# Later feed-forwards on 256 normed columns, and rows placed 64 bytes below the weights

## The chip, the cores and the metric

The kernel runs on one core of a Trainium2 chip. The metric is the device time of one execution in microseconds, as the median of several runs. The trace is that of one further execution, taken by the hardware profiler.

## What is computed

The reference is a two-layer diffusion backbone in float32: 256 latent tokens and 256 context tokens of 1024 channels. Every sub-layer begins with an RMS norm whose rows are scaled and shifted by vectors from a conditioning input (adaLN), and ends with a gated addition to the residual `x`. Layer 0 holds a feed-forward on both streams, a bidirectional state-space mixer and a feed-forward on the latent tokens; layer 1 a feed-forward, a pooling mixer and a feed-forward, all on the latent tokens. The feed-forward, 2816 inner channels wide, is

```
u = rmsnorm(x, g) * (1 + scale) + shift
x = x + 0.5 * gate * ((silu(u @ w_gate) * (u @ w_up)) @ w_down)
```

The adaLN vectors are `silu(c) @ ada_w + ada_b`, nine parts of 1024 per layer.

## The kernel before

**Products.** Channels lie on the partitions and tokens along the columns. The accuracy of float32 is kept by splitting both operands in a high and a low part of a rounded float32 type and making three matmuls, high x high, low x high and high x low (`mm3`, lines 198 to 200): the weights are the stationary operand, the rows the moving one. A product of one output tile of 128 channels is 8 channel tiles x 3 = 24 matmuls into one PSUM bank.

**Weights.** `wsplit` (line 186) loads a block of 128 x 1024 weights by a DMA of SyncE's queue into `raw`, copies it to `hi` on ScalarE (line 192) and subtracts to `lo` on VectorE (line 194). The blocks go round a ring of six buffers: four in pool `wp`, two in `wp0` (first feed-forward) or `wp1` (the later ones). Each of `raw`, `hi` and `lo` takes 4096 bytes of a partition.

**Where tiles lie.** Pools are laid on a stack, each taking as many bytes of every partition as its tiles need, and a pool opened after another was closed may lie over it. `const`, `xres`, `wp`, `tp` and `small` come first and stay (0 to 120128; `wp` from 47296). `u0` with the rows `uh`, `ul` of both streams (2048 bytes a tile) begins at 120128, `wp0` and the pools of the first feed-forward follow it, and later the mixer's pools `scp` and `sd`. When the mixer ends, `u0` is closed too, and `vp` (rows of the later feed-forwards), `fw1`, `fh1` (inner rows `hh`, `hl`, 1024 bytes a tile), `wp1` and `ada1` begin again at 120128, in this order (lines 909 to 916).

**First feed-forward** (`swiglu`, line 273, with the `product` of line 509). Both streams, 512 columns. For each of 22 inner tiles a gate and an up product (`gu`), `gated`, and the split of the result in `hh` (ScalarE) and `hl` (VectorE); then down products (`dn`) from the inner tiles. It takes the inner tiles in blocks of 8, 8 and 6.

**Later feed-forwards** (`ffn`, line 917; 256 latent tokens, three of them). The norm's 1/rms is not ready when the products could start. `Scaled` (line 322) therefore makes rows `vh`, `vl` of `a * x` only, with two more columns that hold the shift, 258 in all (`TV`), and the products run on those. `rbc` is 1/rms on all partitions (line 926). `gated` (line 928) copies the shift's share out of column 256 (`bias`, ScalarE), multiplies the product by `rbc` (line 934, VectorE), and so for gate and up, then applies silu with the bias and the final product. The first four products (tiles 0 and 1) are interleaved by channel (lines 939 to 942); there are four PSUM banks for `gu`, so tile 2 needs a bank that the gate of tile 0 frees. `done` adds each of the 8 output tiles to `x`, adds to the next norm, and makes the next sub-layer's `vh`, `vl`.

**Order.** A tile framework sets the order of each engine's instructions by its own estimate of when they are ready, with the order of the program as priority, and places the semaphores. adaLN parts of layer 1 are computed on VectorE (line 137) beside the first two later feed-forwards, `pace` per product, each from a DMA of 512 KB.

The mixer's products on `u` are `ip` and `pz`; its output product is `op` (rows `yh`, `yl`, 256 columns). The pooling mixer (lines 969 to 1024) uses `vh`, `vl` as stationary operand and keeps four tiles `bq` in `fw1`.

Of the kernel before, what the change touches and what calls it, by code (L numbers as in the profile page):

```python
# [9 lines left out]
F32 = mybir.dt.float32  # L10
# [5 lines left out]
P = 128  # L16
D = 1024
# [9 lines left out]
# columns of the packed per-channel parameters  # L27
# [17 lines left out]
# order of the steps of the first products: x loads 128 tokens, s puts them over their rms, b spreads the conditioning  # L45
# vectors, a loads a channel tile's adaLN weights, c multiplies them, e makes the columns, t turns the tile, m modulates
# it, l loads a weight block, w opens its output, p makes one product
WAVE = "abxxbbbxscpxslesastswssclswlmppattlppeampwcplepwpcmeppaplppatppcpaepwppmcpppwptemcptpepppapppppppppcpppmtppteppppmpm"
# the weight blocks whose low parts GpSimd takes: of the first products, of the mixer's output, gate and input
# [5 lines left out]
# groups of the mixer whose C is made beside the norm  # L55
NC0 = 2
# order of the steps of the mixer's groups: A projections, Z gate, E and D decay factors, B states and outputs,
# O output projection
# [4 lines left out]
def tile_hybrid_backbone(  # L63
# [47 lines left out]
    pk = const.tile([P, C_END], F32, name="pk")  # L111
    cb2 = [const.tile([P, D], F32, name=f"cb{i}") for i in range(2)]
    # context tokens and latent tokens side by side, channels on the partitions
# [44 lines left out]
    def mcol(l, i, part, nm):  # L158
        """The part's vector with its bias, [P, KD]."""
        ada_need(l, part)  # L160
        o = const.tile([P, KD], F32, name=nm)
        a = part * KD
        b0 = C_AB + 72 * l + a
        v.tensor_tensor(o, M[l][:, a : a + KD, i], pk[:, b0 : b0 + KD], op=ALU.add)
        return o

    def scale_cols(l, i, sub, nm):
        """g * (1 + scale) of sub-layer sub."""
# [38 lines left out]
    class Norm:  # L207
# [16 lines left out]
        def rms(self, beside=lambda i: None):  # L224
            """1/rms, tokens on the partitions."""
# [16 lines left out]
        def finish(self, beside=lambda i: None):  # L242
            """1/rms of each token, on all partitions."""
# [9 lines left out]
    def modulate(d, x, rstd, ab, u):  # L253
        """The streams' rows of channel tile d; ab: (tokens, scale column, shift column) of each stream."""
# [18 lines left out]
    def swiglu(l, s, T, product, gated, blocks, hid, nh, done, early):  # L273
        """early: gate and up products of the first hidden tiles, if they are already there."""
# [4 lines left out]
        def gateup(f):  # L279
            if f in early:  # L280
                pt = early.pop(f)
            else:
                pt = []
                for w in range(2):
                    pt.append(product(wsplit(wgu[l, s, w, f])))
                    ada_some()
            h = gated(*pt)
# [24 lines left out]

    def axpy(x, p, g):
# [5 lines left out]
    # -- a * x with the shift as one more column: the tokens' 1/rms comes in behind the products --  # L319
    TV = S + 2  # L320

    class Scaled:
        def __init__(self, l, sub, hs=None, ls=None):
# [5 lines left out]
            h = vp.tile([P, KD, TV], F32R, tag="vh", name="vh")  # L329
            l = vp.tile([P, KD, TV], F32R, tag="vl", name="vl")  # L330
# [16 lines left out]
    # ================= layer 0, first sub-layer =================  # L347
    u = utiles(2 * S)
    with ExitStack() as st:
# [7 lines left out]
        # silu of the conditioning vectors: a column per channel tile, and later all of it on all partitions  # L357
# [21 lines left out]
        def w_x(j):  # L379
            """128 tokens and their rms, tokens on the partitions (where their channels lie later)."""  # L380
# [20 lines left out]
        def w_a(d):  # L401
            """The weights of channel tile d's scales and shifts."""
# [5 lines left out]
        def w_c(d):  # L408
            """Products of the scales, in four parts over the partitions; the shifts."""
# [15 lines left out]
        def w_e(d):  # L425
            """Scale and shift columns."""
# [9 lines left out]
        def w_t(d):  # L436
            """Channels on the partitions."""
# [71 lines left out]
        def product(w):  # L509
# [7 lines left out]
        def gated(pg, pu):  # L517
            sg = tmp("sg", "a")
# [600 lines left out]
```

## Time and profile before

| | |
|---|---|
| median of 3 runs | 1338.82 us (1338.58 to 1342.28) |
| profiled execution, first to last instruction | 1335.9 us |
| TensorE busy | 1279.9 us, 96% of the span |
| VectorE busy | 1023.0 us, 77% |
| ScalarE busy | 609.4 us, 46% |
| GpSimd busy | 150.4 us, 11% |
| read from HBM | 259.96 MB |
| mean granted TensorE clock | 0.992 |

The trace gives the span alone; the runs' times include what lies around it, 2.9 us at the median. Matmuls are pipelined: the next starts before the one ahead has ended, so the busy time of TensorE says that it was occupied, and the distance from one start to the next says how fast it goes.

### The profile page before, as it was taken

How to read it: one execution, taken by the hardware profiler on the slowest of the kernel's cores; microseconds unless marked ns; L12 is line 12 of the kernel's file. 1: busy time of each engine (PE TensorE's matmuls, PEld its weight loads, DVE VectorE, ACT ScalarE, POOL GpSimd, SP SyncE). 2: the span in 40 equal slices, each digit the busy share in tenths (PEclk: the TensorE clock that was granted, in tenths of full speed). 3: DMA queues.
4: the chain of work that ended last, by engine and by line, in shares of the span. 5: the costliest groups of instructions: out<-in, count | busy, mean ns of one | idle time of the engine just before them, and what ended most of it. 6: DMA issues, size and time to landing. Idle time of an engine off the chain costs nothing.

```text
span 1335.9 us, 21101 instructions
## 1 busy us (share of the span) xinstructions
PE 1279.9 (96%) x8246; PEld 1139.1 (85%) x8246; DVE 1023.0 (77%) x1634; ACT 609.4 (46%) x1113; POOL 150.4 (11%) x97
## 2 busy tenths in 40 slices
PE   4999999999999979999988999999999999999997
PEld 3788888888888747788768999999999999999997
DVE  6889988773366879979888898766997667877653
ACT  3243222222235856656535554543645446655541
POOL 4100000000004141434262000000000000000000
PEclk9999999999999989999989999999999999999998
DMA  9387798972232414352332888667886554555551
GB/s 371 133 300 268 243 333 311 309 249 83 77 109 72 176 65 148 114 178 104 127 125 101 319 317 306 200 211 245 291 313 229 168 189 166 180 178 186 163 172 33
DMA packets 74996, 262.46 MB, mean 196 GB/s; under 512 B 8272, under 2 KB 10768, under 8 KB 73872
## 3 DMA queue, kind: packets, MB, share of 16 engines
q1 hardware_dynamic: 74896, 261.11, 57.0%
q8 instruction: 65, 1.06, 0.3%
q14 instruction: 35, 0.29, 0.1%
HBM read 259.96 MB, written 1.11 MB: 195 GB/s over the span
## 4 chain that ended last, share of the span: by engine, by line
PE 78%; DVE 9%; DMA 3%; ACT 3%; POOL 3%; issue 2%; SPq 0%; POOLq 0%; DVEq 0%; ACTq 0%
PE gu L198 15%; PE gu L200 15%; PE gu L199 15%; PE dn L198 8%; PE dn L200 8%; PE dn L199 8%; DVE ca L580 2%; DVE lo L194 2%; POOL em L693 1%; PE py L753 1%; DMA em<-acd 1%; DMA adaw<-in_ada_dram 1%; PE ip L200 1%; PE ip L199 1%; PE po L757 1%
## 5 line engine op out<-in xcount | busy, mean ns | idle before, releaser
L194 DVE TENSOR_TENSOR lo<-raw,hi 128x1024 fp32r<-128x1024 f32 (+1 forms) x312 | 386.0, 1239 | 117.8 <-ACT hi L192 117.2
L192 ACT ACTIVATE hi<-raw 128x1024 fp32r<-128x1024 f32 (+1 forms) x333 | 343.2, 1035 | 265.2 <-PE dn L200 138.5
L198 PE MATMUL gu<-vh,hi 128*128 128x258 f32 x1056 | 299.3, 284 | 0.9 <-DVE sg L934 0.9
L199 PE MATMUL gu<-vh,lo 128*128 128x258 f32 x1056 | 299.7, 284 | 0.0
L200 PE MATMUL gu<-vl,hi 128*128 128x258 f32 x1056 | 297.8, 282 | 0.0
L198 PE MATMUL dn<-hh,hi 128*128 128x256 f32 (+1 forms) x704 | 218.7, 311 | 0.0
L200 PE MATMUL dn<-hl,hi 128*128 128x256 f32 (+1 forms) x704 | 218.7, 311 | 0.0
L199 PE MATMUL dn<-hh,lo 128*128 128x256 f32 (+1 forms) x704 | 218.6, 311 | 0.0
L137 DVE SCALAR_TENSOR_TENSOR junk<-adaw,cb 128x1024 bf16<-128x1024 f32 x152 | 183.6, 1221 | 35.0 <-DMA adaw<-in_ada_dram 34.0
L200 PEld LDWEIGHTS gu<-vl,hi 128*128 128x128 f32 x1056 | 200.4, 190 | 0.0
L198 PEld LDWEIGHTS gu<-vh,hi 128*128 128x128 f32 x1056 | 199.5, 189 | 1.1 <-DVE sg L934 1.1
L199 PEld LDWEIGHTS gu<-vh,lo 128*128 128x128 f32 x1056 | 198.9, 189 | 0.0
L199 PEld LDWEIGHTS dn<-hh,lo 128*128 128x128 f32 x704 | 134.5, 191 | 7.6
L200 PEld LDWEIGHTS dn<-hl,hi 128*128 128x128 f32 x704 | 134.5, 191 | 7.6
L198 PEld LDWEIGHTS dn<-hh,hi 128*128 128x128 f32 x704 | 134.5, 191 | 7.5
L199 PE MATMUL gu<-uh,lo 128*128 128x512 f32 x352 | 139.3, 396 | 1.4 <-POOL lo L194 1.4
L198 PE MATMUL gu<-uh,hi 128*128 128x512 f32 x352 | 140.1, 399 | 0.0
L200 PE MATMUL gu<-ul,hi 128*128 128x512 f32 x352 | 138.4, 397 | 1.5 <-DVE ul L453 1.4
L239 POOL TENSOR_TENSOR rs<-ms,mhalf 128x2 f32<-128x2 f32 (+1 forms) x6 | 6.6, 1094 | 965.4 <-DVE ms L237 965.4
L199 PEld LDWEIGHTS gu<-uh,lo 128*128 128x128 f32 x352 | 66.6, 189 | 17.0 <-POOL lo L194 2.1
L200 PEld LDWEIGHTS gu<-ul,hi 128*128 128x128 f32 x352 | 66.3, 189 | 17.2 <-DVE ul L453 2.2
L198 PEld LDWEIGHTS gu<-uh,hi 128*128 128x128 f32 x352 | 66.7, 190 | 14.8 <-ACT uh L452 0.2
(260 smaller groups left out, 1891.5 us busy)
## 6 DMA issues: line engine op xcount, KB each, us to landing
raw<-in_wgu_dram SPq DMA_DIRECT2D x176, 512.0 KB, 4.7
adaw<-in_ada_dram SPq DMA_DIRECT2D x136, 512.0 KB, 5.0
raw<-in_wd_dram SPq DMA_DIRECT2D x64, 512.0 KB, 3.6
raw<-in_win_dram SPq DMA_DIRECT2D x25, 512.0 KB, 3.3
raw<-in_wd_dram SPq DMA_DIRECT2D x32, 384.0 KB, 3.2
raw<-in_wz_dram SPq DMA_DIRECT2D x16, 512.0 KB, 3.5
em<-acd SPq DMA_DIRECT2D x8, 1024.0 KB, 4.6
raw<-in_wout_dram SPq DMA_DIRECT2D x16, 512.0 KB, 4.2
```

The lines of the kernel that those rows point to most:

```text
L137: v.scalar_tensor_tensor(junk, w, 1.0, cb2[i], op0=ALU.mult, op1=ALU.mult, accum_out=M[l][:, t, i : i + 1])
L192: sc.activation(hi[:, 0:n], r[:, 0:n], AF.Copy)
L194: (sub or v).tensor_tensor(lo[:, 0:n], r[:, 0:n], f32(hi[:, 0:n]), op=ALU.subtract)
L198: pe.matmul(out, wh, xh, start=start, stop=False)
L199: pe.matmul(out, wl, xh, start=False, stop=False)
L200: pe.matmul(out, wh, xl, start=False, stop=stop)
L239: gp.tensor_tensor(r, ms, mhalf[:, 0:n], op=ALU.pow)
L580: v.scalar_tensor_tensor(avw[:, :, lo:hi], ov[:, :, lo + off : hi + off], hw[:, 5 * t + k : 5 * t + k + 1], avw[:, :, lo:hi], op0=ALU.mult ...
L693: gp.tensor_tensor(EM[0][:, :, j, :], EM[0][:, :, j, :], EM[1][:, :, j, :], op=ALU.add)
L753: pe.matmul(py[:, hc], EM[0][:, h, j, :], xl[:, hc], start=True, stop=True)
L757: pe.matmul(po, CT[:, j * P : (j + 1) * P], hin[d][0 if j == d else 1], start=True, stop=True)
```

## The change

Tiles 0 to 2 (`NV = 3`) of a later feed-forward still take the 258 columns of `a * x`. Meanwhile the normed rows `x * rbc * a + b` are made, a product on VectorE and a scaling on GpSimd for each of the 8 channel tiles, in the context half of `XH`, which is free by then. When the products of tile 2 have been issued, `settle` splits them into `vh`, `vl`, over `a * x`, and tiles 3 to 21 (named 4 to 22 when counted from 1) run on 256 columns with the plain gate of the first feed-forward.

Filler tiles (`skip`) and another order of the pools move the rows and some weight blocks: 128 bytes at the head of `u0`, `scp` and `wp1`, 192 at the head of `vp`; `wp1` is opened first, `vp` second, and `fh1` last and anew in each feed-forward. A channel's rows in `vh` and `vl` are 320 floats apart in place of 258. The four `bq` tiles move to the context half of `XH`. Comments and docstrings are taken out.

```diff
+    def skip(pool, nbytes):
+        pool.tile([P, nbytes // 4], F32, name="skip", tag="skip", bufs=1)
...
-                    pt.append(product(wsplit(wgu[l, s, w, f])))
+                    pt.append(product(f, w))
                     ada_some()
-            h = gated(*pt)
+            if f in at_tile:
+                at_tile[f]()
+            h = gated(f, *pt)
...
+    def gate(pg, pu):
+        n = pg.shape[-1]
+        sg = tmp("sg", "a", n)
+        sc.activation(sg, pg, AF.Silu)
+        h = tmp("hf", "b", n)
+        v.tensor_tensor(h, sg, pu, op=ALU.mult)
+        return h
...
-    TV = S + 2
+    TV, TS, NV = S + 2, 320, 3
...
-            h = vp.tile([P, KD, TV], F32R, tag="vh", name="vh")
-            l = vp.tile([P, KD, TV], F32R, tag="vl", name="vl")
+            c = slice(VOFF[0], VOFF.popleft() + TV)
+            h = vp.tile([P, KD, TS], F32R, tag="vh", name="vh")[:, :, c]
+            l = vp.tile([P, KD, TS], F32R, tag="vl", name="vl")[:, :, c]
...
+    skip(upool[0], 128)
     u = utiles(2 * S)
...
+        skip(scp, 128)
...
     st3 = ctx.enter_context(ExitStack())
+    wp1 = st3.enter_context(tc.tile_pool(name="wp1", bufs=2))
+    skip(wp1, 128)
+    rings.extend([wp1] * 2)
     vp = st3.enter_context(tc.tile_pool(name="vp", bufs=1))
+    skip(vp, 192)
     work = st3.enter_context(tc.tile_pool(name="fw1", bufs=1))
-    hid = st3.enter_context(tc.tile_pool(name="fh1", bufs=1))
-    wp1 = st3.enter_context(tc.tile_pool(name="wp1", bufs=2))
-    rings.extend([wp1] * 2)
     adap.append(st3.enter_context(tc.tile_pool(name="ada1", bufs=2)))
+
+    HOFF, VOFF = deque((0, 0, 0)), deque((0, 0, 0, 0))
...
-        ws = [wsplit(wgu[l, s, i % 2, i // 2]) for i in range(4)]
...
+        ws = [wsplit(wgu[l, s, i % 2, i // 2]) for i in range(2 * NV)]
         rbc = vp.tile([P, S], F32, tag="rbc", name="rbc")
         sc.activation(rbc, nrm.finish(), AF.Copy)
+        us = [t[:, 0:S] for t in vec.h], [t[:, 0:S] for t in vec.l]
+        rows = [XH[k][:, ONE] for k in range(KD)]
+
+        def product(f, i):
+            w = ws.pop(0) if ws else wsplit(wgu[l, s, i, f])
+            o = bank("gu", "a")[:, 0 : TV if f < NV else S]
+            for k in range(KD):
+                if f < NV:
+                    vec.cell(o, w, k)
+                else:
+                    prod(o, w, k, us, ONE)
+            return o
+
+        def settle():
+            ws.extend(wsplit(wgu[l, s, i, NV]) for i in range(2))
+            for k in range(KD):
+                sc.activation(us[0][k], rows[k], AF.Copy)
+                v.tensor_tensor(us[1][k], rows[k], f32(us[0][k]), op=ALU.subtract)
+
+        def gated(f, pg, pu):
+            if f >= NV:
+                return gate(pg, pu)
...
+        del ws[0:4]
+        for k in range(KD):
+            v.tensor_tensor(rows[k], X[k], rbc, op=ALU.mult)
+            gp.tensor_scalar(rows[k], rows[k], c1(vec.a, k), c1(vec.b, k), op0=ALU.mult, op1=ALU.add)
...
+        with ExitStack() as sh:
+            hid = sh.enter_context(tc.tile_pool(name="fh1", bufs=1))
...
+            swiglu(l, s, S, product, gated, (NF,), hid, NF, done, early, {NV - 1: settle})
...
-        t = work.tile([P, S], F32, tag="bq", name="bq", bufs=4)
+        t = XH[g][:, ONE]
```

## Rows read from the trace of the kernel before

**Rows 1.** Stages: us, then busy us (x instructions) of each engine, clock, DMA, GB/s.
```profile
65.00:408.50 343.50, 343.50 (x1492) 280.05 (x1490) 253.62 (x410) 100.95 (x134) 0.00 (x0) 1.00 0.65 223
408.50:730.00 321.50, 297.09 (x1552) 234.90 (x1551) 277.10 (x438) 185.72 (x384) 123.55 (x73) 0.98 0.35 121
730.00:860.60 130.60, 128.92 (x1069) 128.53 (x1068) 115.06 (x186) 71.05 (x140) 2.75 (x1) 1.00 0.83 291
```

**Rows 2.** Chain of waits, shares by line: 730 to 1326 us, then 434 to 722.
```profile
by line: PE gu L198 20.6%; PE gu L199 20.5%; PE gu L200 20.3%; PE dn L198 10.3%; PE dn L200 10.3%; PE dn L199 10.3%; DMA adaw<-in_ada_dram 1.8%; issue 0.7%; DVE junk L137 0.7%; DVE lo L194 0.6%; DMA raw<-in_wgu_dram 0.6%; PE pq L198 0.5%; P
...
730.11 3.63 DMA raw<-in_wgu_dram
...
by line: DVE ca L580 8.1%; issue 8.0%; DVE lo L194 6.0%; POOL em L693 5.3%; PE py L753 4.2%; DMA em<-acd 4.1%; PE po L757 3.6%; DVE em L692 3.2%; PE ip L200 3.2%; PE ip L199 3.1%; PE pz L706 3.1%; PE ip L198 3.0%; PE pz L707 3.0%; ACT em L6
```

**Rows 3.** Timeline of TensorE, gate/up: start us, us, engine, line, operation.
```profile
1001.36 0.28 PE L198 MATMUL gu<-vh,hi 128*128 128x258 f32 x1
...
1007.15 0.28 PE L198 MATMUL gu<-vh,hi 128*128 128x258 f32 x1
```

**Rows 4.** The same of a later feed-forward's down products; 50 matmuls from first to last.
```profile
1059.80 0.28 PE L200 MATMUL dn<-hl,hi 128*128 128x256 f32 x1
...
1065.80 0.28 PE L199 MATMUL dn<-hh,lo 128*128 128x256 f32 x1
```

**Rows 5.** The same of the mixer's output products; 58 matmuls from first to last.
```profile
723.23 0.28 PE L199 MATMUL op<-yh,lo 128*128 128x256 f32 x1
...
729.80 0.28 PE L200 MATMUL op<-yl,hi 128*128 128x256 f32 x1
```

**Rows 6.** The same, first feed-forward: first matmuls of products 1, 5 and 7 of seven.
```profile
75.93 0.40 PE L198 MATMUL gu<-uh,hi 128*128 128x512 f32 x1
...
98.24 0.40 PE L198 MATMUL gu<-uh,hi 128*128 128x512 f32 x1
...
109.16 0.40 PE L198 MATMUL gu<-uh,hi 128*128 128x512 f32 x1
```

**Rows 7.** TensorE's groups by line and shape: count, busy us, mean ns of one.
```profile
L198 PE MATMUL gu<-vh,hi 128*128 128x258 f32 x1056 | 299.3, 284 | 0.9 <-DVE sg L934 0.9
...
L198 PE MATMUL dn<-hh,hi 128*128 128x256 f32 x528 | 149.4, 283 | 0.0
...
L198 PE MATMUL ip<-uh,hi 128*128 128x512 f32 x168 | 69.4, 414 | 0.0
...
L706 PE MATMUL pz<-lo,uh 128*128 128x512 f32 x64 | 25.7, 402 | 1.4 <-DVE lo L194 1.4
```

**Rows 8.** Other engines' operations: mean ns; for L261 shortest, median and longest.
```profile
L194 DVE TENSOR_TENSOR lo<-raw,hi 128x1024 fp32r<-128x1024 f32 x181 | 221.0, 1223 | 83.3 <-ACT hi L192 82.9
...
L1009 DVE TENSOR_TENSOR ql<-q,qh 128x256 fp32r<-128x256 f32 x8 | 3.2, 420 | 0.2
...
L1007 ACT ACTIVATE qh<-q 128x256 fp32r<-128x256 f32 x8 | 3.2, 411 | 1.6 <-DVE q L1005 1.5
...
L261 POOL TENSOR_SCALAR mu<-mt,a011a,b x8: 556/810/1917, 414.9 to 429.7; 128x256 f32<-128x256 f32 x8
```

**Rows 9.** Where later feed-forwards begin: timeline rows, `rbc`, products of 1130.8 to 1145.2.
```profile
729.02 0.50 ACT L340 ACTIVATE vh<-x,a02a 128x256 fp32r<-128x256 f32 x1
...
738.21 0.43 PE L249 MATMUL nbc<-cs,rs 128*128 128x128 f32 x2 [1.44 <-POOL rs L239]
...
928.16 0.39 ACT L926 ACTIVATE rbc<-nbc 128x256 f32<-128x256 f32 x1 [2.14 <-PE nbc L249]
...
937.60 0.39 PE L198 MATMUL gu<-vh,hi 128*128 128x258 f32 x1 [0.92 <-DVE sg L934]
...
L926 ACT ACTIVATE rbc<-nbc x3: 385/385/385, 738.7 to 1145.5; 128x256 f32<-128x256 f32 x3
...
L199 PE MATMUL gu<-vh,lo 128*128 128x258 f32 x29 | 8.4, 291 | 0.0
```

More of the change, by code (lines that the diff above doesn't have):

```diff
@@ L270, in tile_hybrid_backbone, with swiglu @@
     ONE = slice(0, S)
-    def swiglu(l, s, T, product, gated, blocks, hid, nh, done, early):
+    def swiglu(l, s, T, product, gated, blocks, hid, nh, done, early, at_tile={}):
         tok = slice(0, T)
@@ L507, in done @@
                 vec.add(d)
-        def product(w):
+        def product(f, i):
+            w = wsplit(wgu[0, 0, i, f])
             if later:
@@ L515, in product @@
             return o
-        def gated(pg, pu):
-            sg = tmp("sg", "a")
-            sc.activation(sg, pg, AF.Silu)
-            h = tmp("hf", "b")
-            v.tensor_tensor(h, sg, pu, op=ALU.mult)
-            return h
+        def gated(f, pg, pu):
+            return gate(pg, pu)
         swiglu(0, 0, 2 * S, product, gated, (8, 8, 6), hid, 9, done, early)
@@ L910, in tile_hybrid_backbone, with product, gated @@
     st3 = ctx.enter_context(ExitStack())
+    wp1 = st3.enter_context(tc.tile_pool(name="wp1", bufs=2))
+    skip(wp1, 128)
+    rings.extend([wp1] * 2)
     vp = st3.enter_context(tc.tile_pool(name="vp", bufs=1))
+    skip(vp, 192)
     work = st3.enter_context(tc.tile_pool(name="fw1", bufs=1))
-    hid = st3.enter_context(tc.tile_pool(name="fh1", bufs=1))
-    wp1 = st3.enter_context(tc.tile_pool(name="wp1", bufs=2))
-    rings.extend([wp1] * 2)
     adap.append(st3.enter_context(tc.tile_pool(name="ada1", bufs=2)))
+    HOFF, VOFF = deque((0, 0, 0)), deque((0, 0, 0, 0))
     def ffn(l, s, sub, nrm, vec, nxt_vec):
-        def product(w):
-            o = bank("gu", "a")[:, 0:TV]
-            for k in range(KD):
-                vec.cell(o, w, k)
-            return o
-        ws = [wsplit(wgu[l, s, i % 2, i // 2]) for i in range(4)]
+        ws = [wsplit(wgu[l, s, i % 2, i // 2]) for i in range(2 * NV)]
         rbc = vp.tile([P, S], F32, tag="rbc", name="rbc")
         sc.activation(rbc, nrm.finish(), AF.Copy)
-        def gated(pg, pu):
+        us = [t[:, 0:S] for t in vec.h], [t[:, 0:S] for t in vec.l]
+        rows = [XH[k][:, ONE] for k in range(KD)]
+        def product(f, i):
+            w = ws.pop(0) if ws else wsplit(wgu[l, s, i, f])
[11 more added lines that the diff above has]
+                v.tensor_tensor(us[1][k], rows[k], f32(us[0][k]), op=ALU.subtract)
+        def gated(f, pg, pu):
+            if f >= NV:
+                return gate(pg, pu)
             bias = small.tile([P, 2], F32, tag="bias", name="bias")
@@ L954, in done @@
                 vn[0].add(d)
-        swiglu(l, s, S, product, gated, (NF,), hid, NF, done, early)
+        with ExitStack() as sh:
+            hid = sh.enter_context(tc.tile_pool(name="fh1", bufs=1))
+            if HOFF[0]:
+                skip(hid, 4 * HOFF[0])
+            HOFF.popleft()
+            swiglu(l, s, S, product, gated, (NF,), hid, NF, done, early, {NV - 1: settle})
         assert not jobs
```

## The prediction, made before the change was run

> **What bounds the kernel now.** I read the stages, then the chain of waits, then single instructions. By stage [rows 1], the first feed-forward (65 to 408.5 us) has TensorE busy without a break, the gate/up half of the first later one (730 to 860.6) for all but 1.7 us, with VectorE below it at 88% and 291 GB/s moving; the mixer (408.5 to 730) leaves TensorE 24 us idle. The chain agrees [rows 2]: from 730 to 1326 six TensorE lines hold 92% of it, gate/up and down products, while in the mixer the products on `u` share it with convolutions, decay factors and transfers. So in the feed-forwards time is the count of matmuls times their **pitch**, start to start. The busy means (284 ns) are of no use here, as neighbours overlap; the pitch comes from the timeline:
> - gate/up, 258 columns: 48 matmuls from 1001.36 to 1007.15 [rows 3], 120.6 ns each
> - down, 256 columns: 50 from 1059.80 to 1065.80 [rows 4], 120.0 ns
> - the mixer's output product, also 256 columns and three passes: 58 from 723.23 to 729.80 [rows 5], 113.3 ns
> - first feed-forward, 512 columns: four products of 24 matmuls from 75.93 to 98.24, 232.4 ns, then two to 109.16, 227.5 ns, 226.7 within the second, and this 4-and-2 pattern repeats through the stage [rows 6]
>
> The last two points are what the change builds on. Down and output products have equal shape, type and passes; what differs is where rows and weights lie. Adding up the pools' tile sizes gives every weight block an offset of 192 (mod 256) except those of `wp0`, at 64. I call rows' offset less weights' offset the distance. Output product: 128-192 = -64, 113.3 ns. Down: 192-192 = 0, 120.0 ns. Gate/up: channel rows 1032 bytes apart, so -128 to -8, 120.6 ns on average. At 512 columns: 64-192 = -128 in the four `wp` blocks of the ring, 64-64 = 0 in the two of `wp0`; the faster two are those at 0.
>
> The Trainium skill speaks against this reading: TensorE: Matmul & The Clock Gate, Step-by-step, gives TensorE two independent read ports, so that loading the next weights takes nothing from the running matmul. By it and its gap of N/2.4 + 2.5 ns an estimate of the whole gain would be 0.8 ns for each matmul that loses two columns, 2.3 us. The trace disagrees by 6.7 ns at equal columns, and the measurement decides; what is left of the rule is the second rival.
>
> **The change, part by part**, matmul counts from [rows 7].
> 1. Gate/up of tiles 3 to 21: 19 x 48 x 3 = 2736 matmuls get 256 columns and distance -64 (`vp` begins 192 higher, rows of 320 floats are 1280 bytes = 5 x 256). From 120.6 to 113.3: **20.0 us** less. Bounds: the output product's 113.3 and the down product's 120.0 (1.6 us); I take the first, as shape and distance are its own.
> 2. Down: 528 x 3 = 1584 matmuls from 0 to -64, 120.0 to 113.3: **10.6 us** less.
> 3. Tiles 0 to 2 keep 258 columns at -64: 432 matmuls. No row shows this; between 113.3 x 258/256 = 114.2 and today's 120.6. I take 114.2, nearest to the output product: **2.8 us**, at worst 0.
> 4. First feed-forward: the 128 bytes move rows and `wp0` blocks to 192, so all distances are 0. The stage's 343.5 us [rows 1] are some 62 products of 24 x 232 ns; 41 of them go from 232.4 to 227.2: 24 x 41 x 5.2 ns = **5.1 us** less. Bounds: 0, and 5.6 if all reach 226.7.
> 5. The mixer's products on `u` also come to 0. Five of their six lines hold 15.4% of its chain of 288 us [rows 2], all six some 18%; 2.2% of 53 us is **1.1 us**. Bounds 0 and 3.4 (696 matmuls x 4.9 ns). The skip in `scp` keeps its other offsets, so the output product stays. The pooling mixer's 120 matmuls go from 0 or mixed to +64, unmeasured: within 5 ns each, 0.6 us either way, taken as 0.
> 6. Gates of tiles 3 to 21 lose two bias copies (ScalarE) and a product with `rbc` (VectorE, 0.42 us by its shape [rows 8]) each. Nothing: TensorE's 5.4 us a tile hides both engines' work before and after.
> 7. Added in each feed-forward: after `rbc`, 8 VectorE products of 0.42 us and 8 GpSimd scalings. Nearest row for the latter: L261, same shape, 0.56 to 1.92 us, median 0.81 [rows 8]. Rows are then done 0.8 + 6.5 us after `rbc`, which starts at 738.7, 928.2 and 1145.5. They are wanted at the end of tile 2, 144 matmuls after the stage begins: about 748, 941.7 and 1154.7 us on the old clock, against 746, 935.5 and 1152.8 [rows 9]. Hidden in all three, by 2 us where it is least; at 1.92 us each (15.4 us) the three would be late by 7, 3 and 7 us. But the products stand ahead of the first gate on VectorE, and that gate frees the bank that tile 2 needs. In the second feed-forward the gate is late anyway, and TensorE already stands 0.92 us there, at 937.60. In the last, 29 rounds of three, some 86 of the first 96 gate/up matmuls, are done when `rbc` comes [rows 9], so 3.4 us of products meet 1.2 us of cover: **+2.2 us**.
> 8. Overwriting `a * x`: 8 copies (ScalarE, 0.41) and 8 subtractions (VectorE, 0.42), each waiting for tile 2's last product to have read its channel, which it leaves every 0.36 us. The eighth is ready 1.3 us after tile 2 ends, and tile 3 wants it 7 x 3 x 0.113 = 2.4 us after. Hidden by 1.1 us; a 1.22-us weight subtraction or adaLN product between them eats that. Queued behind the waiting instructions are the splits of tile 4, wanted 5.4 us later. I take 0.5 each, **+1.5 us**; bounds 0 and 3.8 each (nothing overlapped).
> 9. Six blocks are split ahead of `rbc` rather than four: the ring has six, so only order moves. On SP those loads pass no other kind. Nothing; late next would be `rbc` by two subtractions, 2.4 us.
> 10. Pools: today `wp1` lies over the mixer's pools, and a load into it starts at 730.11 [rows 2], just after the last output product at 729.80 [rows 5]: a new pool waits for the last use of the one beneath. Afterwards `wp1` lies over `u`, free early, but `vp` over the mixer's pools, so no `vh` row can be written at 729.02 [rows 9] any more: shift, copy and subtraction come first, some 1.5 us. Today TensorE loses 1.44 us at 738.21 waiting for the norm [rows 9], which gives most of it back: **+0.7 us**.
>
> DMA carries 6% more per time: 291 becomes 310 GB/s in the stage from 730 [rows 1]; a load has the ring's two tiles of lead. Nothing.
>
> Sum: 20.0 + 10.6 + 2.8 + 5.1 + 1.1 - 2.2 - 1.5 - 0.7 = 35.2 us off the profiled span of 1335.9. The runs' median is 1338.8; the 2.9 us around the span stay. **1303.6, say 1304 us.**
>
> **Rivals.**
> *The rows come late.* GpSimd takes 1.92 us for each, and the overwriting is exposed too: 17 + 11.4 - 1.5 us of further stalls at most, 1331 us; halfway, 1317. For it: L261's spread, with VectorE busy 88% of the stage [rows 1, 8]. Against: its median, and 9 to 13 us between `rbc` and tile 3. By the Trainium skill (SBUF — State Buffer, SBUF: two separate sides) VectorE and GpSimd lock a shared port pair against each other for whole instructions; the spread agrees with that. Chance 0.11.
> *Offsets do nothing.* The output product would be fast for another reason, and only columns count: 2736 x 0.6 ns = 1.6 us gained, 4.4 lost, 1342 us, within 0.3%. This is where the skill's port rule leads. Against: 113.3 and 120.0 at equal shape, and the 4-and-2 pattern that follows the ring. Chance 0.04.
> *The new distance is a bad one.* At 512 columns -128 costs 5.2 ns over 0. If -64 did that to rows in these tiles, 2736 + 432 + 1584 matmuls would go to 125.4: 15.2 + 8.6 us lost, 6.2 gained in parts 4 and 5, 4.4 lost, **1361 us**. It decides once the pitch passes 121.6 (4752 x 1.2 ns + 4.4 - 6.2 = 3.9 us). Against: the output product at that distance. Chance 0.03.
>
> **Numbers.** A measurement here can tell about 0.3%, 4.0 us. Forecast 0.82, late rows 0.11, both faster: 0.93; same 0.04; slower 0.03. The low end is no stall and the mixer's full 3.4: 1338.8 - 41.9 = 1297. The high end reaches halfway into the late rows: 1317. Outside lie the two last rivals, the worse half of the first, and little below.
>
> **What would show it.** Right: gate/up with 256 columns 912 times per line, pitch 113 to 114; down the same; every product of the first feed-forward at 227, the 4-and-2 pattern gone; tile 3 starting without a gap. Wrong: a pitch near 120 in either (then parts 1 and 2 fall), a gap of microseconds ahead of tile 3 put down to ScalarE or VectorE (7, 8), or ahead of the first `vh` product at 730 (10).

## The result and the profile after

The change makes the kernel faster: a median of 1316.47 us over 4 runs (1312.92 to 1321.0) against 1338.7 for the kernel before beside it, a ratio of 0.9832 (95% interval 0.9805 to 0.986). The forecast was 1304, its range 1297 to 1317. Two later series of the changed kernel gave 0.9801 (0.9779 to 0.9823; median 1312.6 of 5) and 0.9834 (0.9817 to 0.9852; 1316.86 of 5). The profiled execution is the slowest of the four, 1321.0 us with a span of 1319.1.

The stages of the kernel after, columns as in [rows 1]: first feed-forward, mixer, gate/up half of the first later feed-forward.

```profile
64.00:407.50 343.50, 339.32 (x1493) 280.52 (x1492) 252.81 (x411) 100.53 (x135) 0.00 (x0) 1.00 0.65 223
407.50:732.40 324.90, 299.26 (x1549) 238.54 (x1548) 279.18 (x434) 184.82 (x379) 123.26 (x73) 0.96 0.37 128
732.40:856.90 124.50, 122.82 (x1067) 122.31 (x1068) 104.38 (x169) 67.55 (x116) 12.66 (x9) 1.00 0.82 284
```

Gate/up takes 124.5 us instead of 130.6. The first feed-forward, though, is as long as before (343.5), now with TensorE idle for 4 us of it, and the mixer is 3.4 us longer. By the ends of the stages' last TensorE products, before and after:

| stage | before | after | difference |
|---|---|---|---|
| first feed-forward | 343.5 | 343.4 | -0.1 |
| mixer | 321.5 | 324.9 | +3.4 |
| first later feed-forward | 194.0 | 184.5 | -9.5 |
| second | 193.0 | 189.4 | -3.6 |
| pooling and third | 208.9 | 203.2 | -5.7 |

The three later feed-forwards get the same edit, and the second gains little more than a third of what the first does. The chain of waits from 732 us still lies on their products, as in [rows 2]:

```profile
by line: PE gu L204 20.4%; PE gu L202 20.4%; PE gu L203 20.4%; PE dn L202 10.5%; PE dn L204 10.5%; PE dn L203 10.5%; DMA adaw<-in_ada_dram 1.0%; issue 0.7%; PE pq L202 0.6%; DVE x L978 0.6%; PE pq L203 0.5%; PE pq L204 0.5%; PE nst L236 0.4
```

So again it is the pitch that has to be read. TensorE's timeline of the kernel after, the first and the 49th of 49 matmuls in a row (the counterparts of [rows 3, 4]): gate/up in the first and second later feed-forward, then down in the first and second.

```profile
799.78 0.28 PE L203 MATMUL gu<-vh,lo 128*128 128x256 f32 x1
...
805.22 0.28 PE L203 MATMUL gu<-vh,lo 128*128 128x256 f32 x1
...
879.79 0.28 PE L204 MATMUL dn<-hl,hi 128*128 128x256 f32 x1
...
885.23 0.28 PE L204 MATMUL dn<-hl,hi 128*128 128x256 f32 x1
...
999.77 0.28 PE L203 MATMUL gu<-vh,lo 128*128 128x256 f32 x1
...
1005.43 0.28 PE L203 MATMUL gu<-vh,lo 128*128 128x256 f32 x1
...
1059.72 0.28 PE L202 MATMUL dn<-hh,hi 128*128 128x256 f32 x1
...
1065.38 0.28 PE L202 MATMUL dn<-hh,hi 128*128 128x256 f32 x1
```

In the first, 5.44 us / 48 = 113.3 ns, gate/up and down alike, as forecast. In the second, 5.66 / 48 = **117.9 ns** for the same instructions at the same distance, from tile 3 to its last down product (the mean over all of them is 117.8). The third runs at 113.3 again. The stage that is slow has 19 x 48 + 528 = 1440 such matmuls: 1440 x 4.45 ns = 6.4 us, which is about what separates a gain of 9.5 from one of 3.6 (5.9).

Counts, as in [rows 7]: the instructions are the forecast ones.

```profile
L202 PE MATMUL gu<-vh,hi 128*128 128x256 f32 x912 | 253.3, 278 | 0.0
...
L202 PE MATMUL gu<-vh,hi 128*128 128x258 f32 x144 | 42.0, 292 | 3.3 <-DVE sg L967 2.6 <-ACT vh L356 0.7
```

First feed-forward, the counterpart of [rows 6]: 105 matmuls apart. 23.80 us / 105 = 226.7 ns; the 4-and-2 pattern is gone.

```profile
74.80 0.39 PE L202 MATMUL gu<-uh,hi 128*128 128x512 f32 x1
...
98.60 0.39 PE L202 MATMUL gu<-uh,hi 128*128 128x512 f32 x1
```

Where the stage lost it again, in the timelines of TensorE and VectorE at 281 us:

```profile
281.30 0.39 PE L204 MATMUL dn<-hl,hi 128*128 128x512 f32 x1
285.87 0.47 PE L202 MATMUL dn<-hh,hi 128*128 128x512 f32 x1 [4.18 <-DVE x L329]
...
283.70 1.22 DVE L141 SCALAR_TENSOR_TENSOR junk<-adaw,cb 128x1024 bf16<-128x1024 f32 x1 [1.08 <-DMA adaw<-in_ada_dram]
...
284.85 0.48 DVE L329 SCALAR_TENSOR_TENSOR x<-dn,g00cg,x 128x256 f32<-128x256 f32 x1
```

TensorE has both `dn` banks full and waits 4.2 us for the first addition to `x` on VectorE (L329). VectorE stands before it at an adaLN product (`junk`), which itself waits 1.08 us for its weights. Then eight matmuls, from 286.53 us on, start 0.43 us apart; the granted clock from 286.2 to 289.4 us is 0.51 in the trace, that is the lower of TensorE's two levels, 1.2 GHz. The kernel before has the same queue with little slack: there the first addition to `x` comes at 285.13 us, also right behind an adaLN product that waits for its weights, and TensorE reaches the same matmul at 286.48 us, 0.9 us after the addition has ended.

```profile
285.13 0.48 DVE L314 SCALAR_TENSOR_TENSOR x<-dn,g00cg,x 128x256 f32<-128x256 f32 x1
```

The starts of the later feed-forwards (the counterpart of [rows 9]), all of TensorE's idle times there that a wait explains, and VectorE's row products of the last:

```profile
733.04 0.40 PE L202 MATMUL gu<-vh,hi 128*128 128x258 f32 x1 [0.70 <-ACT vh L356]
741.08 0.43 PE L253 MATMUL nbc<-cs,rs 128*128 128x128 f32 x2 [0.82 <-POOL rs L243]
754.20 0.39 PE L204 MATMUL gu<-vl,hi 128*128 128x256 f32 x1 [0.22 <-DVE vl L957]
...
936.54 0.38 PE L204 MATMUL gu<-vl,hi 128*128 128x256 f32 x1 [0.78 <-DVE vl L957]
...
1138.61 0.39 PE L202 MATMUL gu<-vh,hi 128*128 128x258 f32 x1 [2.58 <-DVE sg L967]
...
1135.05 3.17 DVE L978 TENSOR_TENSOR x<-x,rbc 128x256 f32<-128x256 f32 x8 [1.72 <-ACT rbc L939]
```

VectorE's order ahead of tile 3 in the second of them:

```profile
934.61 1.21 DVE L198 TENSOR_TENSOR lo<-raw,hi 128x1024 fp32r<-128x1024 f32 x1
...
936.08 2.76 DVE L957 TENSOR_TENSOR vl<-x,vh 128x256 fp32r<-128x256 f32 x8
```

Part 10's wait for `vh` is at 733.04, part 8's at tile 3 are at 754.20 and 936.54, and part 7's is at 1138.61: the eight products on VectorE (3.17 us) stand ahead of the gate that frees tile 2's bank.

GpSimd's row scalings in the three, with shortest, median and longest (the counterpart of the last of [rows 8]):

```profile
L979 POOL TENSOR_SCALAR x<-x,a02a,b x8: 557/1414/1857, 742.5 to 752.3; 128x256 f32<-128x256 f32 x8
L979 POOL TENSOR_SCALAR x<-x,a10a,b x8: 551/864/2832, 923.0 to 930.3; 128x256 f32<-128x256 f32 x8
L979 POOL TENSOR_SCALAR x<-x,a12a,b x8: 555/940/2022, 1135.6 to 1143.5; 128x256 f32<-128x256 f32 x8
```

### The profile page after: what moved, and what is told of

It is laid out like the page before. It is cut to its first block, busy times and chain, and to the rows that moved or that the text cites. A ratio compares the mean times of both kernels' runs of the same rounds, so it can differ in the third digit from the quotient of the medians.

```text
span 1319.1 us, 21138 instructions
## 1 busy us (share of the span) xinstructions
PE 1254.4 (95%) x8246; PEld 1120.4 (85%) x8246; DVE 992.4 (75%) x1568; ACT 597.6 (45%) x1023; POOL 177.1 (13%) x121
## 4 chain that ended last, share of the span: by engine, by line
PE 62%; DVE 18%; DMA 8%; issue 4%; ACT 3%; POOL 3%; SPq 1%; POOLq 0%; DVEq 0%; ACTq 0%
PE gu L204 11%; PE gu L202 11%; PE gu L203 11%; PE dn L202 6%; PE dn L204 6%; PE dn L203 6%; DMA adaw<-in_ada_dram 6%; DVE junk L141 6%; DVE lo L198 3%; DVE ca L595 2%; POOL em L708 1%; PE py L768 1%; DMA em<-acd 1%; PE po L772 1%; PE ip L204 1%
## 5 line engine op out<-in xcount | busy, mean ns | idle before, releaser
L202 PE MATMUL gu<-vh,hi 128*128 128x256 f32 (+1 forms) x1056 | 295.3, 280 | 3.3 <-DVE sg L967 2.6
L204 PE MATMUL gu<-vl,hi 128*128 128x256 f32 (+1 forms) x1056 | 294.8, 280 | 1.0 <-DVE vl L957 1.0
L203 PE MATMUL gu<-vh,lo 128*128 128x256 f32 (+1 forms) x1056 | 294.9, 279 | 0.0
L202 PE MATMUL dn<-hh,hi 128*128 128x256 f32 (+1 forms) x704 | 215.7, 306 | 4.2 <-DVE x L329 4.2
L204 PE MATMUL dn<-hl,hi 128*128 128x256 f32 (+1 forms) x704 | 215.8, 307 | 0.0
L203 PE MATMUL dn<-hh,lo 128*128 128x256 f32 (+1 forms) x704 | 215.7, 306 | 0.0
L296 ACT ACTIVATE hh<-hf 128x256 fp32r<-128x256 f32 (+1 forms) x88 | 40.9, 465 | 88.9 <-DVE hf L325 87.0
```

The costliest lines, as they stand in the source:

```text
L202: pe.matmul(out, wh, xh, start=start, stop=False)
L203: pe.matmul(out, wl, xh, start=False, stop=False)
L204: pe.matmul(out, wh, xl, start=False, stop=stop)
L296: sc.activation(a, h, AF.Copy)
```

## The experiments

All edits are made to the changed kernel, so line numbers are close to those of the kernel after. Pitches are worked out as above.

### Is the slow stage one of two pitches, or noise? The changed kernel twice more

> The changed kernel, run again. Theory (two pitches): a 256-column product at distance -64 runs at 113.3 or at 117.8 ns, which is settled at a stage's entry and holds through it; a whole later feed-forward of 1440 such matmuls differs by 1440 x 4.45 = 6.4 us, so the times gather near 1307, 1313, 1320 and 1326 us (none to three of them at the slow pitch). Rival (one pitch and noise): the times spread evenly about 1316 us, and the trace shows one and the same pitch in a stage whenever it is taken.

> The changed kernel beside it on the same chip. Theory (two pitches): median 1310 to 1318 us, the executions 0, 6.4, 12.8 us (less or more a us for the wait at 281 us) above 1308 to 1309, each later feed-forward of the trace as a whole at 113.3 or 117.8 ns unless a stall cuts it. Rival (one pitch and noise): a spread without steps, and no second pitch in the trace.

Measured: 1309.27, 1309.98, 1312.6, 1316.69 and 1321.27 us, then 1315.45, 1315.71, 1316.86, 1317.21 and 1320.58. The times do not stand in steps; taken alone they would fit an even spread. The traces decide: each later feed-forward from tile 3 on is at 113.3 or at 117.8 ns, but for a few matmuls at its beginning, and at nothing between.

| profiled run | first | second | third | time |
|---|---|---|---|---|
| changed kernel | 113.3 | 117.8 | 113.3 | 1321.0 |
| again (after5) | 117.8 | 113.3 | 117.8 | 1321.27 |
| again (after5b) | 117.8 | 113.3 | 113.3 | 1320.58 |
| ada72, below | 113.3 | 113.3 | 113.3 | 1312.58 |
| gate_first2, below | 113.3 to 752.9 us, then 117.8 | 113.3 | 113.3 | 1312.32 |
| best1, below | 113.3 | 113.3 | 113.3 | 1309.63 |
| best2, below | 117.8 | 113.3 | 113.3 | 1313.54 |

The first later feed-forward, from the mixer's last product to its own, takes 190.7 to 191.4 us in the four runs that have it at 117.8 and 183.9 to 185.3 in the three at 113.3. That a stage keeps what it began with until it stalls, as was expected, does not hold: in the run gate_first2 the pitch changes in the middle of tile 3's products, with no wait in the profile: one matmul starts 0.13 us after the one before instead of 0.11.

```profile
748.03 0.28 PE L202 MATMUL gu<-vh,hi 128*128 128x256 f32 x1
...
752.90 0.29 PE L203 MATMUL gu<-vh,lo 128*128 128x256 f32 x1
753.03 0.28 PE L204 MATMUL gu<-vl,hi 128*128 128x256 f32 x1
...
758.69 0.28 PE L204 MATMUL gu<-vl,hi 128*128 128x256 f32 x1
```

Up to 752.90 it is 4.87 us / 43 = 113.3 ns, from 753.03 on 5.66 / 48 = 117.9. Two other things blur the steps in the totals. The wait at 281 us is different in each run (TensorE idle for 4.2, 1.4 and 2.1 us in the changed kernel's three traces), and the mixer takes 324.9, 322.5 and 325.1 us, with a granted clock between 460 and 500 us of 0.79, 0.91 and 0.87 (0.91 in the kernel before); what sets that clock was not tried.

### Offset or columns? Each alone

```diff
-    HOFF, VOFF = deque((0, 0, 0)), deque((0, 0, 0, 0))
+    HOFF, VOFF = deque((16,) * 3), deque((16,) * 4)
```

> 256 columns kept, the rows at distance 0. Theory (the offset sets the pitch): gate/up and down matmuls of 256 columns at 120.0 ns, 4320 x (120.0 - 113.3) = 28.9 us over a changed kernel without a slow stage (1313): about 1342 us. Rival (the columns alone do it): 113 to 118 ns as in the changed kernel, 1316 us.

```diff
-            o = bank("gu", "a")[:, 0 : TV if f < NV else S]
+            o = bank("gu", "a")[:, 0:TV]
...
-                if f < NV:
-                    vec.cell(o, w, k)
-                else:
-                    prod(o, w, k, us, ONE)
+                vec.cell(o, w, k)
```

(and the rows, `settle` and the plain gate of the later feed-forwards out)

> Placement kept, 258 columns in all inner tiles; no normed rows, no second set of columns. Theory: gate/up at 120.5 to 120.9 ns as before, down at 113.3 or 117.8: the kernel before less 1584 x 6.7 or 2.2 ns, and a wait of about 1 us less or more at the joints: 1329 to 1336 us. Rival (258 columns gain from the offset too, once they run steadily): gate/up near 114.2 ns, 3168 x 6.4 = 20 us more, 1308 to 1316 us.

Measured: columns alone 1336.52 us, ratio 0.9986 (0.9973 to 0.9998); placement alone 1325.6, ratio 0.9905 (0.9885 to 0.9924). TensorE's timeline, 48 matmuls between the two rows of each pair, first of the kernel with columns alone:

```profile
799.76 0.28 PE L203 MATMUL gu<-vh,lo 128*128 128x256 f32 x1
...
805.52 0.28 PE L203 MATMUL gu<-vh,lo 128*128 128x256 f32 x1
...
879.80 0.28 PE L204 MATMUL dn<-hl,hi 128*128 128x256 f32 x1
...
885.56 0.28 PE L204 MATMUL dn<-hl,hi 128*128 128x256 f32 x1
```

5.76 / 48 = 120.0 ns in both. Then placement alone:

```profile
799.77 0.29 PE L203 MATMUL gu<-vh,lo 128*128 128x258 f32 x1
...
805.57 0.29 PE L203 MATMUL gu<-vh,lo 128*128 128x258 f32 x1
...
879.80 0.28 PE L204 MATMUL dn<-hl,hi 128*128 128x256 f32 x1
...
885.45 0.28 PE L204 MATMUL dn<-hl,hi 128*128 128x256 f32 x1
```

258 columns at distance -64: 5.80 / 48 = 120.8 ns, nothing gained over [rows 3]. Down here runs at 117.7 (and at 113.3 in the other two feed-forwards). So the two halves of the change are worth more together than alone: 2.4 and 13.3 us, against 22.5 for both (the median of all 14 runs of the changed kernel is 1316.2). All three kernels (columns, placement, both) also have the new placement in the first feed-forward and the mixer, so the three later feed-forwards by themselves, from the mixer's last product to the last down product of one trace each, say it more sharply: 595.8 us in the kernel before, 597.7 with the columns alone, 587.9 with the placement alone, 577.0, 583.8 and 577.2 with both. There the columns alone gain nothing. Two columns fewer pay only where the offset is right, and in gate/up the offset pays only where there are 256 columns. Both totals came out below their forecasts (1342, and 1329 to 1336), mostly because these left out the first feed-forward: it ran in 338.6 and 340.3 us.

By the Trainium skill (TensorE: Matmul & The Clock Gate, Step-by-step) the moving rows and the next weights come in through two independent read ports, so that loading weights takes nothing from the running matmul. The runs do not bear out that matmuls go equally fast wherever rows and weights lie: with nothing changed but a row offset, the same 256-column matmul takes 120.0 ns or 113.3 to 117.8. What meets what inside is not shown.

All weight blocks of the later feed-forwards lie at 192 (mod 256), so these runs move the rows alone. That the distance counts, and not the rows' own offset, rests on the 512-column products: rows at 64 run at 232.4 and 227 ns with weights at 192 and 64, and rows and weights both at 192 at 226.7.

### Which distances are good? Two maps

```diff
-    HOFF, VOFF = deque((0, 0, 0)), deque((0, 0, 0, 0))
+    HOFF, VOFF = deque((8, 32, 56)), deque((8, 32, 32, 56))
```

(the second map has `(24, 40, 48)` and `(4, 60, 60, 48)`)

> Other distances, 256 columns as in the changed kernel: -32 in the first later feed-forward, +64 in the second, -96 in the third (gate/up from tile 3 on and down alike). Theory (the offset picks which pitches are possible, and the slow 117.8 ns belongs to -64): each distance shows 113.3, 117.8 or 120.0 ns, and one of them may show 113.3 in both its halves. Rival (any distance other than 0 will do): 113.3 or 117.8 ns at all three. A second rival (-64 alone will do): 120.0 ns at all three, which costs 28.9 us over 1313: 1342 us.

> Three more distances: gate/up at -48, -80 and 128, down at +32, +96 and 128 in the three later feed-forwards. Theory: as in the other map, each has 113.3, 117.8 or 120.0 ns; 128 (the 512-column products ran at 232.4 ns there in the kernel before, 226.7 at 0) is a slow one at 120.0. Rival (any distance other than 0): 113.3 or 117.8 ns everywhere, 128 too.

Mean pitch of the 256-column matmuls, from starts less than 0.15 us apart, some 910 of them in gate/up and 527 in down; each distance is that of one feed-forward, but for 0 and -64:

| distance | -96 | -80 | -64 | -48 | -32 | 0 | +32 | +64 | +96 | 128 |
|---|---|---|---|---|---|---|---|---|---|---|
| gate/up, ns | 117.3 | 119.3 | 113.3 or 117.8 | 116.7 | 118.3 | 120.0 | | 117.8 | | 118.7 |
| down, ns | 117.3 | | 113.3 or 117.8 | | 118.3 | 120.0 | 116.7 | 117.8 | 120.0 | 118.7 |

No theory was right in full. The pitch takes more values than three, and it is the same for gate/up and down at equal distance: the distance sets it, not the tile. 113.3 was seen at -64 alone; but most other distances have one feed-forward each (0 has three, all at 120.0), so a second pitch at them is not excluded. Nor does the order carry over to another width: at 512 columns 0 is the fast one (226.7 ns) and 128 the slow one (232.4), at 256 columns 0 and +96 are the slowest of all (120.0). The whole runs took 1328.32 and 1335.7 us.

**High and low rows at different distances.** The low rows `vl` get an offset of their own (and `VOFF` is `(0, 16, 0, 0)`, which puts the high rows of the second at 0):

```diff
+    LOFF = deque((16, -16, 0, 32))
...
+            c = slice(c.start + LOFF[0], c.stop + LOFF.popleft())
             l = vp.tile([P, KD, TS], F32R, tag="vl", name="vl")[:, :, c]
```

> High rows and low rows of the gate/up products at different distances: in the first later feed-forward -64 and 0, in the second 0 and -64, in the third -64 and +64. The low rows are streamed in one matmul of three. Theory (each matmul's own rows and the weights loaded beside it set its pitch): a mean of the parts, near (2 x 113.3 to 117.8 + 120.0) / 3 = 115.5 to 118.5 ns, 117.8 to 119.3 ns, and 114.8 to 117.8 ns. Rival (the pattern locks over the group of three, or the low rows decide the next phase): a pitch of its own outside these, down to 113.3 or up to 120.0 ns.

Measured: 119.3, 117.8 and 117.8 ns (1325.31 us in all). The first lies above its range of means (115.5 to 118.5), the second at the lower end of its own (117.8 to 119.3), the third at the upper end (114.8 to 117.8). A mean of separate matmuls doesn't explain the first, so here the three passes do not simply add up; how they depend on each other was not settled.

### Does adaLN hold the first feed-forward? Eight of its tiles moved

```diff
-        ada_later(1, (0, 1, 2), (0,))
-        pace[0] = 80 / 60
+        ada_later(1, (0, 1), (0,))
+        pace[0] = 72 / 60
```

(the later feed-forwards then take parts 2 to 4, 5 to 7, and 8)

> Eight of the adaLN tiles of the first feed-forward (layer 1, third part) move to the later feed-forwards, the last eight from the second to the third of these. Theory (adaLN on VectorE holds the first feed-forward's end, so its pitch of 226.7 ns gains nothing there): the wait of 4.6 us at 281 us and the half clock behind it shrink, the stage loses 3 to 6 us, the time is 1311 to 1314 us where the changed kernel has 1316.5. Rival (the wait is the down weights' or the accumulators' own): the stage stays at 343 us and the time at 1316 to 1318 us.

Measured: 1315.45 us, ratio 0.9826 (0.9807 to 0.9844). The stretch of the second block's down products, 272.1 to 315.8 us (columns as in [rows 1]):

```profile
272.10:315.80 43.70, 43.70 (x194) 36.24 (x193) 19.04 (x27) 10.13 (x11) 0.00 (x0) 1.00 0.40 131
```

TensorE is busy throughout, and the stage takes 337.3 us where the changed kernel had 343.4, 339.0 and 341.3; the two versions further below with 72 tiles have 337.3 as well. The cause of the wait is shown, and what the placement brings without it: 6.2 us. The total did not follow: the eight tiles in the third later feed-forward put adaLN products ahead of its first gate, whose gap grew from 2.9 to 4.2 us, with three more of 0.8, 0.4 and 1.3 us.

### Placement in the first feed-forward undone

```diff
-    skip(upool[0], 128)
...
-        skip(scp, 128)
```

> The first feed-forward's rows back where they stood before (three quarters of its down products and part of its gate/up at distance 128), the rest as in the changed kernel. Theory (placement alone sets the 512-column pitch): 232.4 ns where the distance is 128, the stage at 343 to 344 us without a wait at 281 us, the time 1.5 to 5 us over the changed kernel's, which lost 0 to 4.6 us of that to the wait: 1314 to 1319 us. Rival (the 512-column pitch came from something else in the change): 226.7 ns throughout and a time of 1312 to 1316 us.

Measured: 1319.04 us, ratio 0.9855 (0.983 to 0.9881). The stage takes 343.5 us with no wait at 281 us, at 232.7 and 226.9 ns by turns, as before. So part 4's mechanism holds, and what it brings in the changed kernel is 0 to 4.5 us, the wait deciding. This run shows by chance a pitch that changes at a stall. VectorE stands at adaLN products of the second later feed-forward, and TensorE waits for the gate behind them:

```profile
1005.43 0.28 PE L202 MATMUL gu<-vh,hi 128*128 128x256 f32 x1
...
1012.41 0.38 PE L202 MATMUL gu<-vh,hi 128*128 128x256 f32 x1 [1.38 <-DVE hf L325]
...
1019.81 0.28 PE L204 MATMUL gu<-vl,hi 128*128 128x256 f32 x1
...
1025.47 0.28 PE L204 MATMUL gu<-vl,hi 128*128 128x256 f32 x1
...
1008.23 1.23 DVE L141 SCALAR_TENSOR_TENSOR junk<-adaw,cb 128x1024 bf16<-128x1024 f32 x1 [2.86 <-DMA adaw<-in_ada_dram]
```

Up to the wait the pitch is 113.3; behind it 5.66 / 48 = 117.9, to the end of the feed-forward. In the run after5b a wait of 1.54 us at 1017.24 left 113.3 as it was. A stall can change the pitch and need not, and the change in gate_first2 shows that none is needed.

### The rows behind the first gate

```diff
-        for k in range(KD):
-            v.tensor_tensor(rows[k], X[k], rbc, op=ALU.mult)
-            gp.tensor_scalar(rows[k], rows[k], c1(vec.a, k), c1(vec.b, k), op0=ALU.mult, op1=ALU.add)
+        def settle0():
+            for k in range(KD):
+                v.tensor_tensor(rows[k], X[k], rbc, op=ALU.mult)
+                e = v if k % 2 else gp
+                e.tensor_scalar(rows[k], rows[k], c1(vec.a, k), c1(vec.b, k), op0=ALU.mult, op1=ALU.add)
...
-            swiglu(l, s, S, product, gated, (NF,), hid, NF, done, early, {NV - 1: settle})
+            swiglu(l, s, S, product, gated, (NF,), hid, NF, done, early, {1: settle0, NV - 1: settle})
```

> The rows' VectorE products and their scale and shift are issued after the first gate instead of ahead of it, and every second scale and shift goes to VectorE instead of GpSimd. Theory (the eight products ahead of the gate hold TensorE in the third later feed-forward, GpSimd's rows hold the joint of tile 3): the gap of 2.9 us at 1135 us and the half clock behind it go (3 to 4 us), the gaps of about 1 us at tile 3 of the first two stay under 0.5 us: 3.5 to 5 us less than the changed kernel's 1312 to 1316: 1308 to 1311 us. Rival (the rows then come late for tile 3, as VectorE begins them 3 us later): a wait of 1 to 4 us at tile 3 in each later feed-forward, and the time stays at 1312 to 1318 us.

Measured: 1310.53 us, ratio 0.9789 (0.9772 to 0.9807). The gap before the gate of the third is gone, but the rival holds there too, if by another wait: tile 3 stands for the low part of its weight blocks (`lo`), which VectorE makes behind the rows. TensorE's timeline of this run:

```profile
1135.86 0.38 PE L203 MATMUL gu<-vh,lo 128*128 128x256 f32 x1 [0.74 <-DVE lo L198]
1137.39 0.38 PE L203 MATMUL gu<-vh,lo 128*128 128x256 f32 x1 [1.15 <-DVE lo L198]
```

From start to start these gaps are 1.1 and 1.5 us, 0.3 more follows, so 2.9 us were moved, not removed. No half clock follows them. In the second feed-forward the joint's gap of 1.1 us is gone, in the first 0.8 at the gate stands for 0.5 at the joint. The range of the theory held, for half of its reasons. The edit also moves half of the scalings to VectorE; the two were not tried apart.

### A version of all three

```diff
-    TV, TS, NV = S + 2, 320, 3
+    TV, TS, NV = S + 2, 320, 4
...
-        ws = [wsplit(wgu[l, s, i % 2, i // 2]) for i in range(2 * NV)]
+        ws = [wsplit(wgu[l, s, i % 2, i // 2]) for i in range(6)]
```

(with the rows behind the gate and 72 adaLN tiles in the first feed-forward; part 8 of layer 1 queued in the third later one's `settle`)

> Tile 3 keeps 258 columns too (256 from tile 4 on), the rows are made after the first gate with every second scale and shift on VectorE, and the first feed-forward has 72 adaLN tiles in place of 80 (the last eight come in the last feed-forward, after its rows are settled). Theory (three separate waits: adaLN at 281 us, the rows ahead of the gate, the rows at the joint): no gap over 0.5 us at the joint in any later feed-forward, none before the gate of the third, none at 281 us; each FF pays 48 x 7.5 = 0.36 us for the fourth tile. Against an execution of the changed kernel with no slow stage (1309) 3 to 5 us less, 1304 to 1306, and 6.4 us more for each slow stage; median 1304 to 1311. Rival (the waits are one chain of VectorE work that only moves, as in the run with the rows after the gate): gaps of the same sum elsewhere, median 1310 to 1315 us.

Measured: 1309.63 us, ratio 0.9802 (0.9779 to 0.9824). The profiled run has no slow stage and still takes 1309.63, so the rival is right for half of it: 0.5 us at most is left at tile 4 and 1.1 before the third's gate, but adaLN stalls appear at 992 (1.6 us) and 1144 us (1.9), and the third waits for the norm. There GpSimd's power of the norm takes 1.61 us while VectorE runs an adaLN product beside it:

```profile
1122.19 1.61 POOL L243 TENSOR_TENSOR rs<-ms,mhalf 128x2 f32<-128x2 f32 x1 [21.62 <-DVE ms L241]
...
1122.03 1.21 DVE L141 SCALAR_TENSOR_TENSOR junk<-adaw,cb 128x1024 bf16<-128x1024 f32 x1
```

In the run with the rows behind the gate VectorE had nothing there, and the same instruction took 0.69 us:

```profile
1126.17 0.69 POOL L243 TENSOR_TENSOR rs<-ms,mhalf 128x2 f32<-128x2 f32 x1 [21.60 <-DVE ms L241]
```

By the Trainium skill (SBUF — State Buffer, SBUF: two separate sides) the two engines lock a shared port pair against each other; both rows agree with that, and so does the spread of the row scalings above. So do the same instructions of the other traces of the changed kernel and its versions: 0.7 us where VectorE is idle or starts after them, 1.6 us where an adaLN product began just before.

The last version puts those eight tiles in the second feed-forward and gives adaLN's weights a third buffer there:

```diff
-    cb2 = [const.tile([P, D], F32, name=f"cb{i}") for i in range(2)]
+    cb2 = [(const, upool[0])[i].tile([P, D], F32, name=f"cb{i}") for i in range(2)]
...
-    adap.append(st3.enter_context(tc.tile_pool(name="ada1", bufs=2)))
+    adap.append(st3.enter_context(tc.tile_pool(name="ada1", bufs=3)))
...
-    ada_later(1, (6, 7, 8), (0,))
+    pace[0] = 32 / 60
+    ada_later(1, (5, 6, 7, 8), (0,))
```

> As the kernel with the fourth tile and 72 adaLN tiles in the first feed-forward, but the last eight adaLN tiles are done in the second later feed-forward (32 there, none in the third), and the later feed-forwards' adaLN weights have three buffers in place of two (the second conditioning vector's copy gives up its place after the mixer for it). Theory (what that kernel gained it lost again to VectorE standing at adaLN products that wait for their weights: 1.6 us at 992 us, 1.9 us at 1124 and 1.9 us at 1144): these go, an execution with no slow stage takes 1303 to 1306 us, the median 1303 to 1310. Rival (adaLN beside the later feed-forwards costs its stalls wherever it stands): stalls of 2 to 5 us in the second later feed-forward, no slow stage 1307 to 1310, median 1308 to 1314 us.

Measured: 1311.63 us (1310.46 to 1315.68), ratio 0.9798 (0.9778 to 0.9817), beside 1316.86 and 0.9834 (0.9817 to 0.9852) for the changed kernel on the same chip. One stage of the profiled run is slow: 1313.54 - 6.4 = 1307.1 without it, the low end of the rival's range, and the median lies in the rival's range too. But the rival's stalls of 2 to 5 us are not there: those in the second feed-forward are down to 0.4 and 0.7 us. Pooling and third take 201.0 us (203.2 and 201.8 in the changed kernel's two traces with the third at 113.3); 1.3 us are left, where the gate's weights wait behind rows on VectorE:

```profile
1138.13 0.39 PE L203 MATMUL gu<-vh,lo 128*128 128x258 f32 x1 [1.26 <-DVE lo L198]
```

The last two versions and the rows behind the gate all beat the kernel before by about 2%. By medians they are 5 to 7 us ahead of the changed kernel's 1316.2, but their intervals overlap or touch its own, so that this lead is likely rather than measured.

## Why the prediction was right and where it was not

The direction held, and so did the mechanism: placement and columns together set the pitch. 1304 was too low, by 12 us against 1316. That the range still holds is in part luck: its upper end of 1317 was set halfway into the late rows, which hardly came, and what filled it is largely a second pitch, inside the bounds of parts 1 and 2 but named by no rival. Five of the 14 runs lie above it.

**Parts 1 and 2** hold the largest share of that. The step that failed is "I take the first, as shape and distance are its own": a single stretch of the output product [rows 5] was taken for the pitch of the distance. The same products of the kernel before run elsewhere at another one, eleven matmuls apart in each pair, 118.2 and then 112.7 ns (about 117.8 and 113.3, given the rounding):

```profile
627.38 0.28 PE L198 MATMUL op<-yh,hi 128*128 128x256 f32 x1
...
628.68 0.28 PE L200 MATMUL op<-yl,hi 128*128 128x256 f32 x1
...
638.82 0.28 PE L198 MATMUL op<-yh,hi 128*128 128x256 f32 x1
...
640.06 0.28 PE L200 MATMUL op<-yl,hi 128*128 128x256 f32 x1
```

So the row for a second state was there before the run. Where the fast pitch held, both terms came as sized (6.7 and 3.5 us of each feed-forward); a slow stage takes 6.4 of these 10.2 back. In the changed kernel's three traces 4 of 9 stages were slow, 4/9 x 3 x 6.4 = 8.5 us. These traces' spans are 18.4 us over the forecast span of 1300.7 on average; of the rest some 3.8 lie in the mixer, 2.8 each in parts 3 and 4, and 0.9 in the half clock behind part 7's wait. Each of the three was the slowest run of its series, so for the median 8.5 is probably too much: 6 of the 21 stages in the table above would make 5.5.

**Part 3** brought nothing: 120.8 ns at 258 columns, the bound called worst. Scaling 113.3 by columns was wrong; the two extra columns cost the whole gain.

**Part 4**: pitch right (226.7), gain given back. The step that failed takes every ns of TensorE's in this stage as a ns of time; VectorE's adaLN queue, which reaches the first addition to `x` at 284.85 us here and at 285.13 in the kernel before, is not in it. Of 5.1 us the three traces show 0.1, 4.5 and 2.2; with eight adaLN tiles fewer it is 6.2, more than the upper bound of 5.6, since the faster third of the products also gains and down was slower than the 4-and-2 pattern (231.3 ns on average against 230.6 in gate/up).

**Part 5**: the products on `u` did become faster, 228.1 ns from start to start on average against 232.6, but no gain is seen in the mixer's time. It scatters by 3 us with the granted clock, more than the 1.1 in question; at the clock of the kernel before (0.91 from 460 to 500 us) it takes 322.5 us against 321.5.

**Part 7**: the right place and close in size, 2.58 us idle for 2.2; not foreseen were some 14 matmuls at half clock behind it, 214 ns apart (granted clock 0.50), 1.3 us, in two of the three traces. GpSimd's median was 0.86 to 1.41 us rather than 0.81. Even so the "late rows" rival is not what held tile 3: the last scalings begin at 752.3, 930.3 and 1143.5 us, and only in the first feed-forward does ScalarE wait for one, for 0.2 us.

**Parts 8 and 10** were right: 0.7, 0.9 and 0 us over the pitch at tile 3 for 1.5, in the second for the reason that part 8 names, a weight subtraction of 1.21 us that stands on VectorE ahead of the eight for `vl` (934.61 us above); at the start of the first, gaps of 1.0 and 1.1 us from start to start replace one of 1.7.

**Rivals.** "Offsets do nothing" fell with the columns alone (1336.52 us at 120.0 ns). "The new distance is a bad one" fell too, though it is two-sided: good or middling.

## What to carry to other kernels

Read a pitch from several stretches, after several stalls, before it enters a sum: a stream of equal matmuls can have more than one, and the average over executions is what counts. A change of operand size and a change of placement may each be worth little and together much, so that trying them one at a time would have dropped the columns and undersold the placement. When TensorE gets faster, look at the queue of the engine that frees its banks: work parked there because it was hidden, here adaLN, becomes the new wait, and moving it only helps where its loads are early.

## What was not expected of the hardware

- Equal matmuls at equal operands' offsets have two pitches, 113.3 and 117.8 ns, mostly kept for a whole stage. A stall of 1.4 us changed the pitch where one of 1.5 us did not, and once it changed with no stall at all. What decides was not found.
- Ten distances (mod 256 bytes) between rows and weights, with the weights at 192 throughout, gave pitches from 113.3 to 120.0 ns at 256 columns, while 258 columns take 120.8 even at -64.
- After TensorE waits of 4.2 and 2.1 us at 281 us the granted clock fell to 0.51 (286.2 to 289.4 us) and 0.54 (285.2 to 288.9); after one of 2.8 us in the same place (placement alone) it stayed at 1.00.
